# A state-space layer before a weight stream: where ScalarE's copies of C, its coefficient copy and two groups of TensorE products stand in the order of work

## The chip, the cores and the metric

The program runs on one core of a Trainium2 chip. Its time is the device time in microseconds (us) of that core, the median of three runs. TensorE is called PE here, VectorE DVE, ScalarE ACT, GpSimd POOL; SP is the engine that issues most DMA transfers. Each engine works through its own instructions strictly in the order in which the program wrote them, and waits at an instruction until what that instruction needs is there.

## What is computed

A decoder trunk of two layers on a sequence of 256 positions with 2048 channels. The first layer is a diagonal complex state-space model (128 groups of 16 channels, 64 states each) with a gated linear unit, then a feed-forward block; the second is dilated attention with a feed-forward block. The change touches the state-space part only:

```
u = rms_norm(x, a_norm_mix);  lb = exp(lam * dt);  f = (lb - 1) / lam
xs[s] = lb * xs[s-1] + (f * B) @ u[s]            # complex state, per group
y = Re(C @ xs) + d * u;  z = gelu(y)
x = x + (z @ w_glu)[:, :2048] * sigmoid((z @ w_glu)[:, 2048:])
x = x + swiglu(rms_norm(x), w_in, w_out)         # and then the second layer
```

## The kernel before, in words

The sequence is cut in 64 chunks of four positions. For the 64 pairs of groups (four *quarters* of 16 pairs, two *halves* of 32) the kernel builds small matrices: W, which takes four inputs into a chunk's end state; K, which takes inputs to outputs within a chunk; T, K laid out for a product with the inputs; and Q, which takes a chunk's start state to its outputs. C stands in the tile `ct` in three parts: minus imaginary, real, imaginary.

All orders are written out by hand. The body of `s5` (from L664) is the order of the state-space layer:

- **POOL**: `c_gain(k)` multiplies quarter k of C by the factor f (three operations of L236 to L238), `scale_u(k)` normalises a quarter of the inputs (L433), `q_build(k)` builds Q of quarter k (twelve operations of the same lines), and `l1([3], pool)` does one level of the scan for quarter 3 (L550 to L553).
- **ACT** copies: after each `c_gain` the negated part of C for that quarter (L465); after every group of transposes `v_trans(u)` the transposed W (L494); after every `v_build(u)` the chunk states `vs` (L509); after `k_build(h)` the matrix K of half h (L528); in `coefs(h, b)` the powers of the decay into a PSUM bank (L575); and the Gelu of the outputs (L634).
- **DVE**: eight times `w_build` (16 operations each, L139), then the scan over chunks: `l1([0, 1])`, `l2(0)`, `l3(0)`, `l3(1)`, `l1([2])`, `l2(1)`, `l3(2)`, `l3(3)` (L550 to L553, and L139 in `l2`). Every step of `l1` and `l3` on DVE reads the coefficients which `coefs` put into PSUM.
- **PE**: for each eighth u the transposes `v_trans(u)` (L151) and the products `v_build` (L505); `k_build(0)` in front of `v_trans(4)` and `k_build(1)` behind `v_build(7)` (L518, L523); `t_part(k)`, products of T with the inputs (L616); `s_part(k)`, products of Q with the scanned states (L628); `z_part(k)`, transposes of the Gelu's output (L151); and between these the first products of the weight stream (`plain`, L792), which `next(st)` advances.
- **SP**: two copies per `scale_u`, sixteen per `t_build(h)` (L536, K into T), and the loads of the weights (L858), 1 MB each, into three buffers that hold W until `k_build` and `v_trans` have read it.

After the state-space layer comes the weight stream: products at full size, with ACT and DVE splitting each weight tile into a high and a low part ahead of them.

Tiles with one tag take turns in a fixed number of buffers, and a new tile is written only after the last reader of the old one in its buffer. `hi` and `lo` have three each. The fourth `hi` tile, `wT[0]` (L472), follows the parameter tile `par`, whose last readers are L331 and L332 on POOL. The fifth `lo` tile, `wT[1]`, follows a tile of small values read last at L334. The fifth `hi` tile, `kt`, follows another tile of small values, read last by `scale_u(3)`.

Of the kernel before, what the change touches and what calls it, by code (L numbers as in the profile page):

```python
# [94 lines left out]
def bc(ap, shape, axes):  # L95
    for a in axes:
        ap = ap.unsqueeze(a)
    return ap.broadcast_to(list(shape))


class Trunk:
# [36 lines left out]
    def tt(self, out, in0, in1, op):  # L138
        self.nc.vector.tensor_tensor(out, in0, in1, op)  # L139
# [227 lines left out]
    def s5(self, st):  # L367
# [3 lines left out]
        upp, usw, bt, ct, vs, za, zb = self.upp, self.usw, self.bt, self.ct, self.vs, self.za, self.zb  # L371
# [33 lines left out]
        def wt(k, q0, n=1):  # L405

            w, q0 = (ws[3][q0 // 8], q0 % 8) if k == 3 else (ws[k], q0)
            return w[:, 128 * q0:128 * (q0 + n)].rearrange("p (q r j c) -> p q r j c", q=n, r=2, j=4)
# [13 lines left out]
        for m in range(2):  # L422
            h = rhs[:, 80 * m:80 * m + 80]
# [16 lines left out]
        fx = self.s5_gain(pool)  # L440
# [12 lines left out]
        def c_mul(o, x, k):  # L453

            qs = slice(16 * k, 16 * k + 16)
            sh = [128, 2, 16, 16]
            v4 = lambda v: v.rearrange("p (r q c) -> p r q c", r=2, q=16)
            self.cmul(pool, o, bc(x[:, 0, qs], sh, [1, 3]), bc(x[:, 1, qs], sh, [1, 3]), ct[:, 1:3, qs], ct[:, 0:2, qs],
                      v4(ptmp[0]), v4(ptmp[1]))

        def c_gain(k):

            qs = slice(16 * k, 16 * k + 16)
            c_mul(ct[:, 1:3, qs], fx, k)
            nc.scalar.activation(ct[:, 0, qs], ct[:, 2, qs], AF.Copy, scale=-1.0)  # L465

        def q_build(k):

            for t in range(4):
                c_mul(qv[k][:, :, :, 16 * t:16 * t + 16], self.lam[:, t, 1:3], k)  # L470
# [27 lines left out]
        def v_build(u):  # L498

            q0, e = 8 * u, u % 2  # L500
            pv = [self.bank(2 + ri) for ri in range(2)]
            for i in range(8):
                for ri in range(2):
                    for g2 in range(2):
                        nc.tensor.matmul(pv[ri][half(g2), 64 * i:64 * i + 64], wT[e][half(ri), i, half(g2)],  # L505
                                         (upp if ri == g2 else usw)[half(ri), q0 + i, 0:64], start=True, stop=True,
                                         tile_position=(64 * ri, 64 * g2))
            for ri in range(2):
                nc.scalar.copy(vs[:, ri, q0:q0 + 8], pv[ri].rearrange("p (q n) -> p q n", q=8))  # L509
# [3 lines left out]
        def k_build(h, bs):  # L513

            kk = [self.bank(b)[:, 0:256] for b in bs]
            c = lambda g2: slice(512 * h + 256 * g2, 512 * h + 256 * g2 + 256)
            for g2 in range(2):
                nc.tensor.matmul(kk[g2], self.ident, dm[:, c(g2)], start=True, stop=False)  # L518
            for i in range(16):
                for ri in range(2):  # L520
                    for i2 in range(2):
                        for g2 in range(2):
                            nc.tensor.matmul(kk[g2][half(i2), 16 * i:16 * i + 16],  # L523
                                             wt(2 * h + i2, i)[half(g2), 0, ri].rearrange("p j c -> p (j c)"),
                                             ct[half(g2), 1 + ri, 32 * h + 16 * i2 + i], start=False,
                                             stop=(i == 15 and ri == 1), tile_position=(64 * g2, 64 * i2))
            for g2 in range(2):
                nc.scalar.copy(kt[:, c(g2)], kk[g2])  # L528

        def t_build(h):  # L530

            for jp in range(4):
                s_ = 16 * (3 - jp)
                for g2 in range(2):
                    for i2 in range(2):
                        nc.sync.dma_start(th[h][64 * g2:64 * g2 + 64 - s_, jp, 256 * i2:256 * i2 + 256],  # L536
                                          kt[64 * i2 + s_:64 * i2 + 64, 512 * h + 256 * g2:512 * h + 256 * g2 + 256])
# [34 lines left out]
        def coefs(h, b):  # L572

            cps[h] = self.bank(b)[:, 0:384].rearrange("p (k r q) -> p k r q", k=4, r=3)
            nc.scalar.copy(cps[h], self.cpa[:, :, :, 32 * h:32 * h + 32])  # L575
# [15 lines left out]
        def l3(k):  # L591

            return pipe([level(k, slice(1, 16), slice(16 * i + 1, 16 * i + 16), i - 1, dve, i) for i in range(1, 4)], True)

        def go(ops, others=()):

            n = 0
            for i, f in enumerate(ops):
                while n < len(others) and n * len(ops) <= i * len(others):
                    others[n]()  # L600
                    n += 1
                f()
            for f in others[n:]:
                f()
# [4 lines left out]
        def t_part(k, bs):  # L609
            py = [self.bank(b) for b in bs]  # L610
            for e in range(2):
                for i in range(4):
                    for h in range(2):
                        q = 16 * k + 8 * e + 4 * h + i
                        for g2 in range(2):
                            nc.tensor.matmul(py[g2][half(h), 64 * (4 * e + i):64 * (4 * e + i) + 64], upp[half(g2), q, 16:80],  # L616
                                             th[k // 2][half(g2), :, 16 * (q % 32):16 * (q % 32) + 16],
                                             start=(e == 0 and i == 0), stop=False, tile_position=(64 * g2, 64 * h))
            return py

        def s_part(k, py):
            for e in range(2):
                for i in range(4):
                    for ri in range(2):
                        for h in range(2):
                            q = 8 * e + 4 * h + i
                            for g2 in range(2):
                                nc.tensor.matmul(py[g2][half(h), 64 * (4 * e + i):64 * (4 * e + i) + 64],  # L628
                                                 vs[half(g2), ri, 16 * k + q], qv[k][half(g2), ri, q], start=False,
                                                 stop=(e == 1 and i == 3 and ri == 1), tile_position=(64 * g2, 64 * h))  # L630
            z = upp[:, 16 * k:16 * k + 16, :].rearrange("p q n -> p (q n)")[:, 0:1024]
            z = z.rearrange("p (j i g c) -> p j i g c", j=4, i=8, g=2)
            for g in range(2):
                nc.scalar.activation(z[:, :, :, g].rearrange("p j i c -> p i j c"),  # L634
                                     py[g].rearrange("p (i j c) -> p i j c", i=8, j=4), AF.Gelu_apprx_tanh)
            zs[k] = z.rearrange("p j i g c -> p j (i g c)")
# [3 lines left out]
        def z_part(k, bs, plain):  # L640

            lo = []
            for e in range(2):
                pt = self.bank(bs[e])
                for j in range(4):
                    self.tr(pt[:, 128 * j:128 * j + 128], zs[k][:, j, 128 * e:128 * e + 128])
                v = lambda x, e=e: x.rearrange("p k (j n) -> p k j n", j=4)[:, 2 * e:2 * e + 2]
                src = pt.rearrange("p (j h n) -> p h j n", j=4, h=2)
                if plain:
                    nc.scalar.copy(v(full(k)), src)  # L650
                else:
                    hi, low = [v(self.zv(k, hl)) for hl in range(2)]
                    nc.scalar.copy(hi, src)
                    lo.append(lambda low=low, src=src, hi=hi: tt(low, src, hi.bitcast(F32), sub))
            return lo
# [11 lines left out]
            scale_u(k)  # L667
        for k in range(2, 4):
            c_gain(k)
        q_build(0)  # L670
        q_build(1)
        for u in range(8):
            go(w_build(u // 2, 8 * (u % 2), 8))
            if u == 4:
                v_build(3)
                k_build(0, (0, 1))
                t_build(0)
                coefs(0, 5)
            v_trans(u, (0, 1))
            if u not in (0, 4):  # L680
                v_build(u - 1)
        v_build(7)
        k_build(1, (2, 3))
        next(st)
        t_build(1)
        go(l1([0, 1], dve))
        py = [t_part(0, (0, 1))]
        py.append(t_part(1, (2, 3)))
        go(l1([3], pool))
        q_build(2)  # L690
        q_build(3)
# [3 lines left out]
        coefs(1, 4)  # L695
        go(l3(0))
        s_part(0, py[0])
        z_part(0, (0, 1), True)
        go(l3(1))
        next(st)  # L700
# [505 lines left out]
```

## Time and profile before

| | us |
|---|---|
| time, median of three runs (2216.51 to 2218.11) | 2217.62 |
| the profiled execution's own time | 2219.6 |
| its span, first to last instruction | 2217.8 |
| PE busy in the span | 2130.8 (96%) |
| DVE busy | 1523.4 (69%) |
| ACT busy | 1000.5 (45%) |
| POOL busy | 202.9 (9%) |

A busy share is a mean over the whole span, and most of the span is the weight stream. The state-space layer lies in about the first 157 us. The page cuts the span into 40 slices of 55.4 us; PE's busy tenths there are 0, 7, 9, 9 and so on, those of POOL 8, 8, 2, 1 and then 0. The mean granted TensorE clock of the execution is 0.990 of full speed.

### The profile page before, as it was taken

How to read it: one execution, taken by the hardware profiler on the slowest of the kernel's cores; microseconds unless marked ns; L12 is line 12 of the kernel's file. 1: busy time of each engine (PE TensorE's matmuls, PEld its weight loads, DVE VectorE, ACT ScalarE, POOL GpSimd, SP SyncE). 2: the span in 40 equal slices, each digit the busy share in tenths (PEclk: the TensorE clock that was granted, in tenths of full speed). 3: DMA queues.
4: the chain of work that ended last, by engine and by line, in shares of the span. 5: the costliest groups of instructions: out<-in, count | busy, mean ns of one | idle time of the engine just before them, and what ended most of it. 6: DMA issues, size and time to landing. Idle time of an engine off the chain costs nothing.

```text
span 2217.8 us, 28488 instructions
## 1 busy us (share of the span) xinstructions
PE 2130.8 (96%) x11132; PEld 1757.3 (79%) x11132; DVE 1523.4 (69%) x2621; ACT 1000.5 (45%) x1159; POOL 202.9 (9%) x180
## 2 busy tenths in 40 slices
PE   0799999999999999999999999999999999999998
PEld 0658888888888888878888888878888888888886
DVE  6686777677767764655776676687767776774544
ACT  2324444444444443434445555545444444444443
POOL 8821000000000000000000000000000000000000
PEclk9799999999999999999999999999999999999999
DMA  5235555555555555555554354445555555555553
GB/s 179 84 137 201 183 201 190 206 190 188 196 190 196 189 202 191 180 198 184 205 181 161 142 185 148 152 164 197 190 193 190 190 197 200 190 210 206 192 190 133
DMA packets 66839, 404.69 MB, mean 182 GB/s; under 512 B 15248, under 2 KB 16784, under 8 KB 19088
## 3 DMA queue, kind: packets, MB, share of 16 engines
q1 hardware_dynamic: 65696, 397.12, 50.9%
q10 hardware_dynamic: 720, 4.18, 0.5%
q8 instruction: 87, 1.43, 0.3%
q0 software_dynamic: 288, 1.57, 0.2%
q14 instruction: 48, 0.39, 0.1%
HBM read 397.34 MB, written 2.10 MB: 180 GB/s over the span
## 4 chain that ended last, share of the span: by engine, by line
PE 89%; DVE 6%; issue 2%; POOL 2%; ACT 1%; DMA 0%; ACTq 0%; POOLq 0%
PE b L778 28%; PE b L781 28%; PE b L777 28%; DVE scr L871 2%; DVE lo L139 1%; PE b L792 1%; PE b L151 1%; PE b L1094 1%; ACT hi L755 1%; PE b L1125 1%; POOL xw L433 1%; PE b L628 0%; PE b L1096 0%; PE b L1095 0%; DVE b L139 0%
## 5 line engine op out<-in xcount | busy, mean ns | idle before, releaser
L148 DVE SCALAR_TENSOR_TENSOR lo<-raw,gcol,hi 128x1024 fp32r<-128x1024 f32 x464 | 594.5, 1291 | 324.7 <-ACT hi L759 318.8
L777 PE MATMUL b<-hi,xt 128*128 128x512 f32 x1856 | 727.6, 392 | 1.3 <-ACT hi L759 1.3
L778 PE MATMUL b<-lo,xt 128*128 128x512 f32 x1856 | 724.2, 390 | 0.9 <-DVE lo L148 0.9
L759 ACT ACTIVATE hi<-raw,gcol 128x1024 fp32r<-128x1024 f32 x464 | 525.1, 1148 | 399.1 <-PE b L781 379.6
L781 PE MATMUL b<-hi,xt 128*128 128x512 f32 x1856 | 572.9, 390 | 0.0
L139 DVE TENSOR_TENSOR lo<-raw,hi 128x1024 fp32r<-128x1024 f32 x264 | 327.4, 1246 | 283.5 <-ACT hi L755 278.6
L755 ACT CAST hi<-raw 128x1024 fp32r<-128x1024 f32 x264 | 275.0, 1052 | 303.0 <-PE b L781 293.6
L781 PEld LDWEIGHTS b<-hi,xt 128*128 128x128 f32 x1856 | 349.1, 188 | 72.9
L777 PEld LDWEIGHTS b<-hi,xt 128*128 128x128 f32 x1856 | 348.8, 188 | 73.2 <-ACT hi L759 1.8
L778 PEld LDWEIGHTS b<-lo,xt 128*128 128x128 f32 x1856 | 349.3, 188 | 71.9 <-DVE lo L148 1.6
L778 PE MATMUL b<-lo,ht 128*128 128x512 f32 x704 | 274.7, 390 | 2.5 <-DVE lo L139 2.5
L777 PE MATMUL b<-hi,ht 128*128 128x512 f32 x704 | 274.4, 390 | 0.1
L871 DVE STREAM_TRANSPOSE scr<-scr 32x128 f32<-32x128 f32 x704 | 212.9, 302 | 11.4
L781 PE MATMUL b<-hi,ht 128*128 128x512 f32 x704 | 217.4, 390 | 0.0
L778 PEld LDWEIGHTS b<-lo,ht 128*128 128x128 f32 x704 | 132.3, 188 | 31.3 <-DVE lo L139 4.1
L777 PEld LDWEIGHTS b<-hi,ht 128*128 128x128 f32 x704 | 132.2, 188 | 27.8 <-ACT hi L755 0.5
L781 PEld LDWEIGHTS b<-hi,ht 128*128 128x128 f32 x704 | 132.2, 188 | 27.3
L875 POOL TENSOR_TENSOR ht<-scr,ht 128x512 fp32r<-128x512 f32 x44 | 57.0, 1295 | 880.9 <-ACT ht L874 880.9
L874 ACT CAST ht<-scr 128x512 fp32r<-128x512 f32 x44 | 27.3, 621 | 178.6 <-DVE scr L871 178.6
L871 DVE STREAM_TRANSPOSE scr<-x 32x128 f32<-32x128 f32 x320 | 96.8, 302 | 4.9
L875 POOL TENSOR_TENSOR xt<-scr,xt 128x512 fp32r<-128x512 f32 x20 | 25.9, 1294 | 769.9 <-ACT xt L874 642.0
L778 PE MATMUL b<-lo,z 128*128 128x512 f32 x224 | 87.7, 392 | 0.6 <-DVE lo L139 0.6
(207 smaller groups left out, 1463.1 us busy)
## 6 DMA issues: line engine op xcount, KB each, us to landing
raw<-in_fi SPq DMA_DIRECT2D x176, 1024.0 KB, 4.7
raw<-in_fo SPq DMA_DIRECT2D x88, 1024.0 KB, 4.7
raw<-in_wq SPq DMA_DIRECT2D x48, 1024.0 KB, 4.7
raw<-in_glu SPq DMA_DIRECT2D x32, 1024.0 KB, 4.8
raw<-in_wo SPq DMA_DIRECT2D x16, 1024.0 KB, 4.8
raw<-in_kv SPq DMA_DIRECT2D x8, 1024.0 KB, 4.7
xw<-in_xu SPq DMA_DIRECT2D x4, 640.0 KB, 11.1
qp<-in_xr SPq DMA_DIRECT2D x4, 512.0 KB, 9.7
```

The source lines that it names most:

```text
L139: self.nc.vector.tensor_tensor(out, in0, in1, op)
L148: self.nc.vector.scalar_tensor_tensor(out, in0, s, in1, op0, op1)
L151: self.nc.tensor.transpose(out, in_, self.ident[:n, :n])
L433: pool.tensor_tensor(upp[:, qs, :], upp[:, qs, :], bc(rt, [128, 16, 80], [1]), mul)
L755: nc.scalar.copy(hi, raw)
L759: nc.scalar.activation(hi, raw, AF.Copy, scale=gk)
L777: nc.tensor.matmul(ps[b], xh, hi[:, c], start=first, stop=False)
L778: nc.tensor.matmul(ps[b], xh, lo[:, c], start=False, stop=False)
L781: nc.tensor.matmul(ps[b], xl, hi[:, c], start=False, stop=last)
L871: nc.vector.transpose(out[32 * q:32 * q + 32, :, 32 * a:32 * a + 32], src[32 * a:32 * a + 32, :, q, :])
L874: nc.scalar.copy(dst(0), out)
L875: nc.gpsimd.tensor_tensor(dst(1), out, dst(0).bitcast(F32), ALU.subtract)
```

## The change

`c_gain` no longer has its ACT copy. A new function `c_turn(h)` makes the copies of two quarters in one instruction; its two calls stand behind `t_build(0)` and behind `v_build(7)`. `q_build(0)` and `q_build(1)` are written behind `c_turn(1)`. `coefs(0, 5)` moves from u = 4 to u = 2. On PE `t_part(0)` stands ahead of `k_build(1)`, and `t_part(1)` behind `s_part(0)`.

```diff
         def c_gain(k):
 
-            qs = slice(16 * k, 16 * k + 16)
-            c_mul(ct[:, 1:3, qs], fx, k)
+            c_mul(ct[:, 1:3, 16 * k:16 * k + 16], fx, k)
+
+        def c_turn(h):
+
+            qs = slice(32 * h, 32 * h + 32)
             nc.scalar.activation(ct[:, 0, qs], ct[:, 2, qs], AF.Copy, scale=-1.0)
...
         for k in range(2, 4):
             c_gain(k)
-        q_build(0)
-        q_build(1)
         for u in range(8):
             go(w_build(u // 2, 8 * (u % 2), 8))
             if u == 4:
                 v_build(3)
                 k_build(0, (0, 1))
                 t_build(0)
-                coefs(0, 5)
+                c_turn(0)
             v_trans(u, (0, 1))
             if u not in (0, 4):
                 v_build(u - 1)
+            if u == 2:
+                coefs(0, 5)
         v_build(7)
+        c_turn(1)
+        q_build(0)
+        q_build(1)
+        py = [t_part(0, (0, 1))]
         k_build(1, (2, 3))
         next(st)
         t_build(1)
         go(l1([0, 1], dve))
-        py = [t_part(0, (0, 1))]
-        py.append(t_part(1, (2, 3)))
         go(l1([3], pool))
...
         s_part(0, py[0])
+        py.append(t_part(1, (2, 3)))
         z_part(0, (0, 1), True)
```

## Rows read from the trace of the kernel before

**Rows 1.** Waits, 15 to 160 us: who waited for whom, total, times, longest (us).

```profile
DVE b L550 <- ACT b L575: 28.8, 1, 28.8
ACT z L465 <- POOL z L238: 26.7, 4, 12.0
```

**Rows 2.** Timeline of ACT: start, us, engine, line, operation, [idle before <- releaser].

```profile
52.37 0.42 ACT L465 ACTIVATE z<-z 128x256 f32<-128x256 f32 x1 [3.07 <-POOL z L238]
52.69 1.05 ACT L494 COPY hi<-b 128x512 f32<-128x512 f32 x2
...
64.81 1.07 ACT L509 COPY vs<-b 128x512 f32<-128x512 f32 x2 [1.17 <-PE b L505]
72.03 0.65 ACT L528 COPY hi<-b 128x256 f32<-128x256 f32 x2 [6.15 <-PE b L523]
72.56 0.50 ACT L575 COPY b<-scr 128x384 f32<-128x384 f32 x1
```

**Rows 3.** Timeline of DVE.

```profile
43.60 0.75 DVE L139 TENSOR_TENSOR z<-b,hi 128x256 f32<-128x256 f32 x2
73.10 0.70 DVE L550 TENSOR_TENSOR b<-b,vs 128x512 f32<-128x512 f32 x1 [28.76 <-ACT b L575]
...
108.18 0.67 DVE L550 TENSOR_TENSOR b<-b,vs 128x480 f32<-128x480 f32 x1
...
123.71 0.27 DVE L139 TENSOR_TENSOR b<-b,vs 128x64 f32<-128x64 f32 x1
...
143.82 0.66 DVE L553 TENSOR_TENSOR vs<-b,hi 128x480 f32<-128x480 f32 x1
```

**Rows 4.** Timeline of PE.

```profile
85.02 1.19 PE L518 MATMUL b<-lo,cst 128*128 128x256 f32 x4 [0.60 <-ACT vs L509]
...
95.47 3.84 PE L616 MATMUL b<-tz,xw 64*64 64x64 f32 x126
108.29 3.71 PE L628 MATMUL b<-qp,vs 64*64 64x64 f32 x128 [8.99 <-DVE vs L553]
113.17 1.97 PE L151 MATMUL b<-cst,xw 128*128 128x128 f32 x8 [1.18 <-ACT xw L634]
...
119.75 2.10 PE L628 MATMUL b<-qp,vs 64*64 64x64 f32 x128
...
144.74 2.09 PE L628 MATMUL b<-qp,vs 64*64 64x64 f32 x127
148.49 0.27 PE L628 MATMUL b<-qp,vs 64*64 64x64 f32 x1 [1.66 <-issue]
...
154.88 2.05 PE L628 MATMUL b<-qp,vs 64*64 64x64 f32 x128
```

**Rows 5.** Timeline of POOL.

```profile
31.30 0.45 POOL L332 TENSOR_TENSOR lo<-hi,lo 128x128 f32<-128x128 f32 x1
...
39.76 5.72 POOL L433 TENSOR_TENSOR xw<-xw,hi 128x1280 f32<-128x1280 f32 x2
...
53.43 1.06 POOL L237 TENSOR_TENSOR lo<-scr,z 128x512 f32<-128x512 f32 x1
...
79.08 1.29 POOL L238 TENSOR_TENSOR qp<-lo 128x512 f32<-128x512 f32 x1
85.60 1.05 POOL L550 TENSOR_TENSOR lo<-scr,vs 128x512 f32<-128x512 f32 x1 [5.23 <-ACT vs L509]
...
98.16 1.20 POOL L553 TENSOR_TENSOR vs<-lo 128x480 f32<-128x480 f32 x1
...
126.14 1.27 POOL L238 TENSOR_TENSOR qp<-lo 128x512 f32<-128x512 f32 x1
```

**Rows 6.** Timeline of SP: issues of the first sixteen copies of K.

```profile
72.43 12.03 SPq L536 DMA_DIRECT2D tz<-hi  x16
```

**Rows 7.** DMA issues by line: count, KB each, median us from issue to landing.

```profile
tz<-hi SPq DMA_DIRECT2D x8, 64.0 KB, 2.0
```

**Rows 8.** By stretch: us, busy time of each engine, granted clock, DMA share, GB/s.

```profile
108.30:113.00 4.70, 3.70 (x128) 3.51 (x128) 4.63 (x9) 0.96 (x2) 4.46 (x5) 0.50 0.08 17
```

## The prediction

> **What bounds the kernel now.** I read the 40 slices first: PE is busy nine tenths and more from the third slice on, so the weight stream is bound by PE, and nothing in the change touches an instruction of it. What the change can move is the moment at which the stream takes over, some 157 us after the start. So I took the waits of 15 to 160 us next. Two of them are long [rows 1]: DVE waits 28.8 us, once, for the coefficients that ACT copies, and ACT waits 26.7 us, in four pieces, for POOL's products of C. The timelines show that they are one chain. ACT's copy for quarter 3 of C (52.37 us) waits for POOL, and the copies of W stand behind it and begin at 52.69; from there PE, ACT and PE again go through transposes, states and K, until ACT, behind the copies of K (72.03 + 0.65), copies the coefficients at 72.56 [rows 2]. DVE has built the last W at 43.60 + 0.75 = 44.35 and stands until 73.10 [rows 3]. From 73.10 it runs without a gap through l1, l2(0) and l3(0), and s_part(0) on PE starts at 108.29, released by DVE after 8.99 us of idle time [rows 4]. So POOL's products of C hold ACT, ACT holds DVE, DVE holds PE, and PE starts the rest late.
>
> **The change part by part.**
>
> *The copies of C leave ACT's queue ahead of W.* The first copy of W no longer waits for 52.37 + 0.42. The next thing that it waits for is its buffer: `wT[0]` takes the one of `par`, read last on POOL by L332, which ends at 31.30 + 0.45 = 31.75 [rows 5]. So the copies of W begin at about 31.8, which is 52.69 - 31.75 = 20.9 earlier. PE's and ACT's work from there is the same, and I shift it as it stands: the states of v_build(3), copied by 64.81 + 1.07 = 65.88 [rows 2], are there at 45.0. Their operands don't hold them: DVE finishes all eight parts of W at 44.35, when only the fourth is used here, and quarters 0 and 1 of the inputs stand ahead of L332 in POOL's order. k_build(0) then needs quarter 1 of C, finished when POOL goes on to the next row at 39.76 [rows 5]; PE gets there at 64.81 - 20.9 = 43.9.
>
> *The coefficients at u = 2.* They add their 0.50 [rows 2] to ACT between two copies that PE waits for; I add all of it: states of v_build(3) at 45.4, copies of K at 72.68 - 20.9 + 0.5 = 52.2. DVE finds the coefficients ready when it has built W at 44.35. It needs the states of quarter 0 first and those of quarter 1 only with its fourth operation, some 1.8 us later (46.2, operations of about 0.6), after 45.4. So its scan starts at 44.35 in place of 73.10, **28.75 us earlier**, and this is the main term [rows 3]. Nothing on DVE can give more, since the 44.35 stays.
>
> *c_turn.* Half of C in one copy lies between the 0.42 of a quarter and the 1.05 of two tiles of 512 columns; I take 0.6, nearest to half of the latter [rows 2]. c_turn(0) ends at 52.2 + 0.6 = 52.8. It adds a wait to POOL: q_build(0) is behind it, and with q_build(0) all that POOL does later. The first operation of q_build(0) that reads the negated part started at 53.43 [rows 5], so it loses nothing, with 0.6 us to spare. c_turn(1), behind v_build(7), is needed by q_build(2) alone, far later.
>
> *POOL after that.* q_build(1) ends where it did, 79.08 + 1.29 = 80.37. Then l1 of quarter 3 waited 5.23 us, until 85.60, for the states of v_build(7); these come 20.4 earlier (20.9 less the coefficients' 0.5), at 65.2, and the wait goes. l1 takes 98.16 + 1.20 - 85.60 = 13.76 and ends at 94.1. DVE's l2(1) needs it; its start moves from 123.71 to 94.96 [rows 3, 5]. The cover is thin, 0.8 us, but it holds. q_build(3) ends at 126.14 + 1.27 - 5.23 = 122.2; s_part(3), moved by some 28 from 154.88 [rows 4, 5], needs it at about 127.
>
> *t_part(0) ahead of k_build(1).* On PE this adds a wait for SP's sixteen copies of K. They took 12.03 us to issue and the large ones land after 2.0 [rows 6, 7]: from 52.2 to 64.3, landed at 66.3. The states of v_build(7), which PE waited for until 85.02, come 20.4 earlier, at 64.6, so PE stands some 2 us. Behind it are k_build(1), then the third weight load and the second sixteen copies on SP. t_part(0) takes half of the pair's 3.84, 1.9; k_build(1) with its start took 95.47 - 85.02 = 10.45, a pause of PE's own in it. It ends at 66.3 + 1.9 + 10.45 = 78.7, and s_part(0) can start at 108.29 - 28.75 = 79.5 [rows 4]. So this costs nothing, by 0.8 us; without that cover each us later costs one.
>
> *t_part(1) behind s_part(0).* It lay in PE's idle time; now 1.9 us stand on PE's path, beside a wait of 1.18 for the Gelu [rows 4]. So 0.74 is added, between 0 (quick products, which the Gelu covers whole) and 1.9 (if the Gelu is late by as much). z_part(0) is behind it, and behind that the first weight products.
>
> *From s_part(0) to the stream* PE hardly stands, and its instructions are the same. l3(2) ends at 143.82 + 0.66 = 144.48 - 28.75 = 115.7; PE, which reached s_part(2) at 144.74, gets there at 144.74 - 28.75 + 0.74 = 116.7 [rows 3, 4]. So PE sets this, by 1.0, and the sum is -28.75 + 0.74 = **-28.0 us**.
>
> This sum takes s_part(0) at its slow length: 3.71, where s_part(1) takes 2.10, with a granted clock of 0.50 from 108.30 to 113.00, the lower level of 1.2 GHz, after 9 us in which PE stood [rows 4, 8]. In the changed kernel PE stands less before it. The Trainium skill, page "TensorE: Matmul & The Clock Gate", Part 1, says that "the default state is throttled, and activity releases the throttle". By that rule s_part(0) may run at 2.4 GHz; by the row it ran at 1.2 after an idle stretch longer than the one that I expect, so the row leaves it open, and I make it a rival.
>
> The profiled execution took 2219.6, the span of 2217.8 and 1.8 around it; that is 2.0 above the median of 2217.62. 2219.6 - 28.0 = 2191.6, and by the median **2189.6**.
>
> **The rivals.**
>
> *A quicker clock at s_part(0).* If s_part(0) takes 2.10 and t_part(1) hides behind the Gelu, PE comes to s_part(2) at least 1.61 + 0.74 sooner. But then l3(2) is late: s_part(2) starts at 115.7 and not before, 144.74 - 115.7 = 29.0 saved, 2188.6. For it: less idle time before. Against: 0.8 us of pause and whatever slow stretch k_build(1) itself has. If the pause of 1.66 that PE makes at the end of s_part(2) [rows 4] went too, it would be 30.7, 2186.9, the bottom of what I can construct.
>
> *POOL becomes the bound.* If PE pauses in k_build(0), or waits there for more of C than it reads, c_turn(0) comes late. From 55.2 on (53.43, the cover of 0.8 and the 1.0 by which DVE is ahead of PE) each us costs one. If k_build(0) had to wait for quarter 3 of C, 52.4 in place of 43.9 [rows 2], c_turn(0) would end at 52.8 + 8.5 = 61.3: 6.1 lost, -21.9, 2195.7. For it: the covers are thin. Against: DVE's l1 of quarters 0 and 1 ran from 73.10 [rows 3] while states of later quarters in the same tile were being written, so waits follow the part that is read.
>
> *The copies of W don't start at 31.8.* If their buffers were held until scale_u(3) has read its factors, at 39.76 + 5.72 = 45.48 [rows 5], 13.7 later, the states of quarter 1 would come at 45.4 + 13.7 = 59.1, where DVE wants them at 46.2: 12.9 lost, -15.1, 2202.5. By the count of three buffers it is `kt` that waits for that reader, and not `wT`.
>
> *The wait on DVE stays*, if something else of that chain holds the states until 73: then no more than t_part(1)'s 0.74 is changed, 2218.4.
>
> *Slower: q_build behind c_turn(0).* POOL's whole rest, 28 us of q_build, 13.8 of l1 and 28 of q_build, now hangs on one ACT copy that is queued behind the copies of K. From 55.2 on it eats the gain, and from 55.2 + 28.0, about 83, the kernel is slower. If it were done only after k_build(1)'s end of before, 95.5 + 0.6 = 96.1 [rows 4], the kernel would be 12.9 slower, 2230.5. Against: even at the times of before the copies of K ended at 72.68 [rows 2], ten us short of that point.
>
> **How the numbers follow.** My forecast 0.66, quicker clock 0.14, POOL as the bound 0.10, late copies of W 0.05, the wait stays 0.03, slower 0.02. The range is 2186.5 to 2196.0: it holds the first three, 0.90 together, less what the sizes in them leave uncertain, about 0.8. Below it is only the bottom of the second; 2196.0 takes in thin covers that fail by up to 6 us. A measurement of this kernel tells 0.2%, 4.4 us, from no change: faster 0.95, same 0.03, slower 0.02.
>
> **What would show it.** DVE's first L550 near 44.4 in place of 73.1, with no wait for L575; the first W copy of ACT near 31.8; POOL's first L237 of q_build still near 53.4; no 5.23 before POOL's L550, and l2(1) near 95; PE with a wait before t_part(0) at about 64 to 66, k_build(1) done before 79.5, s_part(0) released by DVE at 79.5 and then t_part(1). From s_part(2) on all should lie some 28 us earlier. I am wrong if DVE still waits before l1, if PE comes late to s_part(0) because of k_build(1), or if l2(1) waits for POOL.

## The result, and the profile after

The changed kernel takes 2192.55 us (median of four runs, 2190.69 to 2192.97) against 2217.79 for the kernel before (four runs, 2216.51 to 2218.11): a ratio of 0.9886, 95% interval 0.9869 to 0.9903, 25.2 us faster. The forecast was 28.0 faster, at 2189.6, with a range from 2186.5 to 2196.0. The profiled execution took 2192.67, with a span of 2190.9; the one of the kernel before took 2219.6, with a span of 2217.8. By either number these two executions differ by 26.9.

The chain that was to break is broken at its first link. This is ACT's timeline, which answers to [rows 2] (line numbers have moved, by 3 up to the Gelu and by 6 in the weight stream: L497 was L494, L512 was L509, L531 was L528, L553 to L556 were L550 to L553, L578 was L575, L619 was L616, L631 was L628, L798 was L792; L468 is `c_turn`).

```profile
31.81 1.07 ACT L497 COPY hi<-b 128x512 f32<-128x512 f32 x2 [7.36 <-POOL lo L332]
...
39.57 0.50 ACT L578 COPY b<-scr 128x384 f32<-128x384 f32 x1
...
43.21 1.07 ACT L512 COPY vs<-b 128x512 f32<-128x512 f32 x2 [1.17 <-PE b L508]
50.53 0.65 ACT L531 COPY hi<-b 128x256 f32<-128x256 f32 x2 [6.25 <-PE b L526]
51.06 0.65 ACT L468 ACTIVATE z<-z 128x512 f32<-128x512 f32 x1
```

The copies of W start at 31.81 in place of 52.69, and what they now wait for is L332 on POOL, the last reader of the buffer. The coefficients are there at 40.1, the states of v_build(3) at 44.3. DVE's timeline answers to [rows 3]:

```profile
43.63 0.74 DVE L139 TENSOR_TENSOR z<-b,hi 128x256 f32<-128x256 f32 x2
44.48 0.70 DVE L553 TENSOR_TENSOR b<-b,vs 128x512 f32<-128x512 f32 x1
...
95.22 0.27 DVE L139 TENSOR_TENSOR b<-b,vs 128x64 f32<-128x64 f32 x1
...
115.39 0.66 DVE L556 TENSOR_TENSOR vs<-b,hi 128x480 f32<-128x480 f32 x1
```

The wait of 28.76 us is gone: no bracket stands behind the first L553. POOL, to be held against [rows 5], has lost its wait of 5.23 in front of l1 (L553, L550 before). Up to there its work lies within 0.3 us of where it was, and behind it everything is some 5 us earlier:

```profile
53.59 1.06 POOL L237 TENSOR_TENSOR lo<-scr,z 128x512 f32<-128x512 f32 x1
...
80.63 1.06 POOL L553 TENSOR_TENSOR lo<-scr,vs 128x512 f32<-128x512 f32 x1
...
93.22 1.21 POOL L556 TENSOR_TENSOR vs<-lo 128x480 f32<-128x480 f32 x1
```

PE's timeline, beside [rows 4]:

```profile
63.84 1.28 PE L619 MATMUL b<-tz,xw 64*64 64x64 f32 x62 [0.36 <-DMA tz<-hi]
...
79.80 3.69 PE L631 MATMUL b<-qp,vs 64*64 64x64 f32 x128 [3.48 <-DVE vs L556]
83.24 1.46 PE L619 MATMUL b<-tz,xw 64*64 64x64 f32 x64
84.67 1.09 PE L151 MATMUL b<-cst,xw 128*128 128x128 f32 x8
86.00 3.70 PE L798 MATMUL b<-raw,xw 128*128 128x512 f32 x8 [0.24 <-ACT xw L653]
...
116.19 2.09 PE L631 MATMUL b<-qp,vs 64*64 64x64 f32 x127 [1.50 <-DVE vs L556]
119.47 0.27 PE L631 MATMUL b<-qp,vs 64*64 64x64 f32 x1 [1.20 <-issue]
120.43 1.09 PE L151 MATMUL b<-cst,xw 128*128 128x128 f32 x8 [0.69 <-ACT xw L637]
121.36 5.29 PE L798 MATMUL b<-raw,xw 128*128 128x512 f32 x8
126.58 1.16 PE L619 MATMUL b<-tz,xw 64*64 64x64 f32 x64
127.56 2.05 PE L631 MATMUL b<-qp,vs 64*64 64x64 f32 x128
129.54 0.50 PE L783 MATMUL b<-hi,z 128*128 128x512 f32 x1
```

Three more rows of the kernel before belong beside these: the weight products behind s_part(0) and behind s_part(2), and the first product of the weight stream.

```profile
114.97 4.86 PE L792 MATMUL b<-raw,xw 128*128 128x512 f32 x8
...
150.37 3.60 PE L792 MATMUL b<-raw,xw 128*128 128x512 f32 x8
...
156.86 0.50 PE L777 MATMUL b<-hi,z 128*128 128x512 f32 x1
```

s_part(0) starts 28.49 us earlier than before, s_part(2) 28.55, the transposes behind it 29.01, but s_part(3) only 27.32 (154.88 less 127.56). What differs between the last two is one row: eight weight products that take 5.29 us, where the same eight took 3.60 before. The views by stretch show why; the columns are those of [rows 8], the granted clock the number in front of the DMA share. First the kernel before, then the changed one:

```profile
149.40:150.30 0.90, 0.86 (x8) 0.86 (x9) 0.87 (x2) 0.11 (x1) 0.00 (x0) 1.00 0.09 18
150.30:153.90 3.60, 3.60 (x11) 1.41 (x8) 3.33 (x5) 2.85 (x4) 0.00 (x0) 1.00 0.00 0
```

```profile
79.80:83.50 3.70, 3.70 (x140) 3.70 (x143) 3.63 (x7) 0.00 (x0) 3.62 (x4) 0.50 0.40 117
83.50:86.00 2.50, 2.26 (x72) 1.92 (x66) 2.43 (x5) 1.72 (x4) 2.34 (x3) 0.90 0.23 59
...
119.40:121.30 1.90, 1.14 (x9) 1.01 (x10) 1.87 (x4) 0.70 (x2) 1.82 (x3) 1.00 0.03 9
121.30:126.60 5.30, 5.30 (x14) 2.00 (x11) 5.20 (x8) 2.86 (x4) 1.18 (x1) 0.68 0.00 0
```

The clock comes up sooner behind s_part(0), in 83.5 to 86.0, and falls for a part of 121.3 to 126.6 (0.50 in 122.5 to 124.0), after PE stood three times in a row: 1.50 for DVE, 1.20 of its own, 0.69 for the Gelu. From s_part(3) on the two executions run side by side again: the stream starts 27.32 earlier (129.54 for 156.86) and takes 0.4 longer, which leaves 26.9 at the end of the span.

### The profile page after: what moved, and what is told of

It is laid out like the page before. It is cut to its first block, busy times and chain, and to the rows that moved or that the text cites. A ratio compares the mean times of both kernels' runs of the same rounds, so it can differ in the third digit from the quotient of the medians.

```text
span 2190.9 us, 28487 instructions
## 1 busy us (share of the span) xinstructions
PE 2129.8 (97%) x11132; PEld 1754.8 (80%) x11132; DVE 1523.6 (70%) x2621; ACT 999.6 (46%) x1157; POOL 203.6 (9%) x180
## 4 chain that ended last, share of the span: by engine, by line
PE 88%; DVE 9%; issue 2%; ACT 1%; DMA 0%; ACTq 0%; DVEq 0%
PE b L784 28%; PE b L783 28%; PE b L787 28%; DVE scr L877 2%; DVE lo L139 1%; DVE b L139 1%; PE b L151 1%; PE b L1100 1%; ACT hi L761 1%; DVE b L553 1%; PE b L1131 1%; DVE b L555 1%; DVE vs L556 1%; DVE hi L554 0%; DVE hi L139 0%
## 5 line engine op out<-in xcount | busy, mean ns | idle before, releaser
L880 ACT CAST ht<-scr 128x512 fp32r<-128x512 f32 x44 | 27.3, 621 | 178.6 <-DVE scr L877 178.6
```

Source lines behind the costliest of these rows:

```text
L880: nc.scalar.copy(dst(0), out)
```

## The experiments

All are edits of the changed kernel, timed against the kernel before on the same chip. That kernel's median was 2218.60 beside the runs whose labels begin with `a_` to `d_`, 2218.12 beside `e_turn_late`, `g_w_sixteen` and `dg_both`, and 2219.02 beside `h_half_first` and `gh_both`. The ratios' intervals are about 0.0015 to either side, some 3 us: runs that lie within 3 us of each other are told apart by the rows of their traces, not by their times. Each trace is one execution.

**The coefficients late again** (`a_coefs_late`)

```diff
                 t_build(0)
+                coefs(0, 5)
                 c_turn(0)
...
-            if u == 2:
-                coefs(0, 5)
```

> The changed kernel with one part undone: coefs(0, 5) stands behind the copies of K again, ahead of c_turn(0). My theory (DVE's first scan step waits for the later of W, states and coefficients, and the whole rest follows DVE): the copies of K end at 50.7, the coefficients at 51.2, the scan starts there and not at 44.5, so 6.7 us are lost, 2199.3. Rival, the copies of C alone bring the gain: the time of the changed kernel, 2192.6.

Measured: 2200.78, ratio 0.9919 (0.9906 to 0.9933). DVE's timeline:

```profile
51.58 0.70 DVE L553 TENSOR_TENSOR b<-b,vs 128x512 f32<-128x512 f32 x1 [7.19 <-ACT b L578]
```

The scan starts 7.1 later than in the changed kernel (6.7 expected), and s_part(0) (86.82) and s_part(2) (123.22) are 7.0 later. The profiled execution, 2199.98, is 7.3 above that of the changed kernel. The rival, that the copies of C alone bring the gain, would have left 2192.6: it falls.

**The copies of C back in ACT's queue** (`b_copies_back`)

```diff
             c_mul(ct[:, 1:3, 16 * k:16 * k + 16], fx, k)
+            qs = slice(16 * k, 16 * k + 16)
+            nc.scalar.activation(ct[:, 0, qs], ct[:, 2, qs], AF.Copy, scale=-1.0)
...
-                c_turn(0)
...
-        c_turn(1)
```

> The changed kernel with the negated copies of C back in c_gain, a quarter at a time, and without c_turn; the coefficients stay early. My theory: ACT's copies of W wait for POOL until 52.7 again, the states of quarter 1 come at 65.2, and the fourth scan operation runs there in place of 46.3: 18.9 us are lost, 2211.5. Rival, the early coefficients alone bring the gain: 2192.6.

Measured: 2212.28, ratio 0.9968 (0.9955 to 0.9980).

```profile
61.82 0.70 DVE L555 TENSOR_TENSOR b<-b,vs 128x512 f32<-128x512 f32 x1 [17.49 <-ACT b L580]
...
66.03 0.70 DVE L555 TENSOR_TENSOR b<-b,vs 128x512 f32<-128x512 f32 x1 [2.32 <-ACT vs L514]
```

The first operation waits for the coefficients, which ACT now delivers at 61.8, and the fourth for the states, which come at 66.0: 19.7 later than the fourth operation at 46.28 in the changed kernel. s_part(0) starts at 99.52, 19.7 later too. So neither edit does it alone: coefficients early without the copies moved give about 6 of the 25 us, copies moved without early coefficients about 18.

**The T products where they were** (`c_t_order_back`)

```diff
-        py = [t_part(0, (0, 1))]
         k_build(1, (2, 3))
...
         go(l1([0, 1], dve))
+        py = [t_part(0, (0, 1))]
+        py.append(t_part(1, (2, 3)))
...
         s_part(0, py[0])
-        py.append(t_part(1, (2, 3)))
```

> The changed kernel with both t_part behind k_build(1) and ahead of s_part(0) again. My theory: no difference beyond 1 us, 2191.6 to 2193.6, since k_build(1) with its pauses still ends ahead of the scan's 79.8 and s_part(2) waits for DVE anyway. Rival, the order of the T products is part of the gain: k_build(1) and both t_part end behind 79.8 and s_part(0) is late by 1 to 3 us, 2194 to 2196.

Measured: 2191.83, ratio 0.9877 (0.9864 to 0.9891): the same, as far as this can tell. The rows show that two things cancel.

```profile
76.09 3.94 PE L619 MATMUL b<-tz,xw 64*64 64x64 f32 x126
79.81 0.35 PE L631 MATMUL b<-qp,vs 64*64 64x64 f32 x9
83.06 3.48 PE L631 MATMUL b<-qp,vs 64*64 64x64 f32 x119 [2.89 <-issue]
...
117.66 2.09 PE L631 MATMUL b<-qp,vs 64*64 64x64 f32 x127
...
122.93 3.60 PE L798 MATMUL b<-raw,xw 128*128 128x512 f32 x8
```

Both t_part end at 80.0, just in time. But a pause of PE's own, 2.89, now falls into s_part(0), which ends at 86.54, 3.05 later than in the changed kernel. So far the rival is right. The changed kernel has no such pause there; why it comes here is not shown. s_part(2) comes at 117.66, 1.5 later, without a wait for DVE; behind it the clock stays at 1.00 (122.9 to 126.5), the weight products take 3.60, and s_part(3) starts at 127.44, within 0.12 of the changed kernel. So in these two executions the order of the T products is worth nothing at the end of the stage, though my reason (s_part(2) waits for DVE anyway) was not what happened.

**c_turn(0) late** (`e_turn_late`)

```diff
-                c_turn(0)
...
+        c_turn(0)
         v_build(7)
         c_turn(1)
```

> The changed kernel with c_turn(0) put in front of v_build(7), so that it ends at 62.2 and not at 51.7. This tests the cover on POOL. My theory: the first read of the negated part in q_build(0) moves from 53.6 to 62.2, POOL's l1 of quarter 3 ends 8.6 later, at 103.0, and DVE's l2(1), with 0.8 us of cover, starts at 103.1 in place of 95.2; nothing behind it takes that up, so 7.8 us are lost, 2200.4. Rival, POOL is hidden (it is 9% busy): 2192.6.

Measured: 2200.15, ratio 0.9918 (0.9905 to 0.9932). POOL's timeline, then DVE's:

```profile
63.52 1.06 POOL L237 TENSOR_TENSOR lo<-scr,z 128x512 f32<-128x512 f32 x1 [9.90 <-ACT z L468]
...
103.10 1.20 POOL L556 TENSOR_TENSOR vs<-lo 128x480 f32<-128x480 f32 x1
```

```profile
104.33 0.28 DVE L139 TENSOR_TENSOR b<-b,vs 128x64 f32<-128x64 f32 x1 [9.27 <-POOL vs L556]
```

POOL, busy in 9% of the span, stops the kernel: the copy came 1.3 later than I had reckoned, l2(1) is 9.1 late and s_part(2) (125.25) as well. 1.1 of it comes back: the weight products behind s_part(2) take 3.60 in place of 5.29 (1.69), 0.97 less lies between s_part(2) and the transposes, where PE's own pause of 1.20 is not there, and s_part(2) itself, at a granted clock of 0.54, takes 3.61 in place of 2.09 (1.52 lost); s_part(3) at 135.48 is 7.9 late. That the time comes so near to the 2200.4 expected is in part luck: the 1.3 too much and the 1.1 that came back nearly cancel.

**The last weight step ahead of s_part(2)** (`d_weights_first`)

```diff
+        next(st)
         s_part(2, py[2])
...
         lo = z_part(2, (2, 3), False)
-        next(st)
```

> The changed kernel with the last step of unsplit weight products (n = 7) put ahead of s_part(2), where PE stood 1.5 us for DVE. My theory (the wait for l3(2) and the pauses behind it are PE time lost, and the granted clock fell behind them): s_part(2) starts at 118.2 without a wait, the stream at 127.1 in place of 129.5, so 2190.2, with the clock at its upper level all through. Rival: the pause between s_part(2) and z_part(2) is longer without these products, the clock falls all the same: 2192 to 2193.

Measured: 2189.12, ratio 0.9865 (0.9850 to 0.9881).

```profile
117.75 2.10 PE L631 MATMUL b<-qp,vs 64*64 64x64 f32 x128
121.03 1.09 PE L151 MATMUL b<-cst,xw 128*128 128x128 f32 x8 [1.19 <-ACT xw L637]
...
123.52 1.70 PE L619 MATMUL b<-tz,xw 64*64 64x64 f32 x59 [1.07 <-DVE vs L556]
```

```profile
123.50:125.00 1.50, 1.48 (x61) 1.48 (x65) 1.15 (x2) 1.26 (x2) 0.00 (x0) 0.59 0.00 0
125.00:128.10 3.10, 3.10 (x141) 3.03 (x135) 2.41 (x4) 0.00 (x0) 0.00 (x0) 0.65 0.24 53
```

The wait in front is gone and the stream starts at 128.02 in place of 129.54, but not at the 127.1 that I expected: without weight products behind s_part(2) PE stands 1.19 there and again until DVE's scan ends, and the clock falls all the same. On this the rival was right; the time is below both, 1.1 under my 2190.2 and 2.9 under the rival's 2192.

**W in wider operations** (`g_w_sixteen`), and both edits together (`dg_both`)

```diff
-            go(w_build(u // 2, 8 * (u % 2), 8))
+            if u >= 6:
+                go(w_build(3, 8 * (u % 2), 8))
+            elif u % 2 == 0:
+                go(w_build(u // 2, 0, 16))
```

> The changed kernel with W of quarters 0 to 2 built by operations of 512 columns in place of two of 256 each (same numbers of W). By 0.60 for 512 columns and 0.335 for 256, DVE is done 1.9 us sooner, at 42.5, and the scan starts there. My theory: s_part(0) moves by 1.9, but l2(1) then waits for POOL's l1 of quarter 3, which stays at 94.4, so only 0.8 us reach s_part(2): 2191.7. Rival, DVE alone sets the rest: 1.9 us, 2190.6.

> The weight products ahead of s_part(2) and W in operations of 512 columns, both. My theory: behind s_part(2) the T products of quarter 3 wait for the end of DVE's scan, which POOL lets come 0.8 us sooner: 0.8 below the run with the weight products moved alone (2189.1), so 2188.3. Rival, DVE alone: 1.9 below it, 2187.2.

Measured: 2188.93 (2188.20 to 2191.13), ratio 0.9870 (0.9856 to 0.9883), and 2190.12, ratio 0.9873 (0.9859 to 0.9886). DVE's timeline in the first:

```profile
40.81 0.74 DVE L139 TENSOR_TENSOR z<-b,hi 128x256 f32<-128x256 f32 x2
...
44.54 0.70 DVE L553 TENSOR_TENSOR b<-b,vs 128x512 f32<-128x512 f32 x1 [0.98 <-ACT vs L512]
...
94.18 0.27 DVE L139 TENSOR_TENSOR b<-b,vs 128x64 f32<-128x64 f32 x1 [0.73 <-POOL vs L556]
```

DVE is done with W 2.8 us sooner (41.55; 1.9 expected), then waits 0.98 for the states of quarter 1 and 0.73 for POOL. s_part(0) starts at 78.13, 1.7 earlier, and s_part(2) at 115.11, 1.1 earlier. So POOL passes on 1.1, nearer to my 0.8 than to the rival's 1.9. In the profiled execution the clock fell here as well, already in s_part(2) (0.62 in 115.1 to 118.3, 0.50 behind it), and the stream starts at 128.40, the same 1.1 earlier; its time is the 2191.13, and the others lie 2 to 3 us below. Their median is 2.8 under the 2191.7 expected and 1.7 under the rival's, and no row shows why. With both edits the stream starts at 127.01 (0.2 before what I expected), yet the time is 1.8 above the 2188.3 expected; from its start to the end of the span the stream took 2061.1 there and 2060.3 with the weight step moved alone, and what that 0.8 is stays open. The same stretch took 2061.4 in the changed kernel and 2060.9 in the kernel before, so differences of this size come with any two executions compared here.

**The last weight step cut in two** (`h_half_first`), and with W in wider operations (`gh_both`)

```diff
+        next(st)
         s_part(2, py[2])
...
-        for n in range(2, self.PLAIN):
+        for n in range(2, self.PLAIN - 1):
             plain(n, (0, 1))
             yield
+        for m in range(2):
+            plain(self.PLAIN - 1, (m,))
+            yield
```

> The changed kernel with the last unsplit step of weight products (n = 7) cut in two: the products for the first 128 positions ahead of s_part(2), those for the second behind z_part(2). My theory (the clock fell because PE stood before s_part(2) and again behind it, and an idle stretch of PE filled on both sides keeps it up): 1.8 us of products fill the 1.5 in front of s_part(2) and 1.8 the time until DVE's scan ends at 123.5; s_part(2) at 116.5, s_part(3) at 124.7, the stream from 126.8, against 129.5 in the changed kernel and 128.0 with the whole step in front: 2188.9 for an execution with the clock at 1.00 from 113 to 129. Rival, the clock falls by chance of the moment and not for the idle time: 2190 to 2192 with a stretch at 0.50.

> The same with W in operations of 512 columns. My theory: POOL lets 0.8 us of DVE's gain through, so the stream starts at 126.0, 2188.1. Rival, PE sets the end of this stretch by then: as the run with the step cut in two alone.

Measured: 2189.47 (2188.66 to 2189.60), ratio 0.9867 (0.9850 to 0.9883), and 2188.05 (2187.85 to 2188.88), ratio 0.9861 (0.9846 to 0.9876). The first by stretch and on PE:

```profile
112.00:129.00 17.00, 15.14 (x353) 10.24 (x352) 14.96 (x23) 6.07 (x9) 10.36 (x10) 1.00 0.47 156
```

```profile
116.87 2.10 PE L631 MATMUL b<-qp,vs 64*64 64x64 f32 x128
120.16 1.09 PE L151 MATMUL b<-cst,xw 128*128 128x128 f32 x8 [1.19 <-ACT xw L637]
121.08 1.88 PE L799 MATMUL b<-raw,xw 128*128 128x512 f32 x4
```

With work on both sides of s_part(2) the clock stays at its upper level, 2.4 GHz, all through, and the stream starts at 126.84, which is the 126.8 expected. Its profiled execution took 2188.66, 0.2 below what I had written; the other three took 2189.43 to 2189.60, and were not traced, so whether the clock held in them is not known. The median does not tell this run from the one with the whole step in front (2189.12); the 1.2 between them is read from two traces.

In the second the stream starts at 125.96 (126.0 expected), and PE still stands three times:

```profile
115.54 2.09 PE L631 MATMUL b<-qp,vs 64*64 64x64 f32 x128 [1.19 <-DVE vs L556]
118.81 1.09 PE L151 MATMUL b<-cst,xw 128*128 128x128 f32 x8 [1.18 <-ACT xw L637]
...
123.01 1.10 PE L619 MATMUL b<-tz,xw 64*64 64x64 f32 x59 [1.07 <-DVE vs L556]
```

```profile
112.00:128.00 16.00, 12.56 (x347) 9.02 (x346) 14.21 (x22) 5.99 (x9) 10.11 (x10) 1.00 0.35 122
```

These stops add up to 3.4 us, as do the three of the changed kernel (1.50, 1.20, 0.69), and the clock stays at 1.00: here half a weight step, 1.88, lies between the second and the third. Its median is 31.0 us below the kernel before, the lowest of all that ran; its interval overlaps those of its neighbours and that of the changed kernel.

## Why the prediction was right

*The copies of C.* Right. 31.8 was forecast for the first copy of W, 31.81 measured, released by L332 as the count of buffers said; so "the copies of W don't start at 31.8" falls, and "the wait on DVE stays" with it.

*The main term.* Right: 44.35 forecast, 44.48 measured. The runs with either edit undone show that the scan goes on only when both the coefficients and the states are there, and that the rest follows it.

*c_turn and POOL.* Right: 0.65 for 0.6, done at 51.7 for 52.8; q_build reads at 53.59, l1 of quarter 3 ends at 94.43 for 94.1, l2(1) starts at 95.22 for 94.96. The cover of 0.8 is what the trace has, and the run with c_turn(0) late shows the price behind it. The rival "POOL becomes the bound" and the one that ends slower rest on this mechanism, and it exists; only the point from which it decides was not reached. That point lies sooner than the 55.2 of the prediction: of its terms the 1.0 by which DVE was to be ahead of PE is not there (see below), which leaves 53.59 + 0.79 = 54.4. With c_turn(0) late the first read came at 63.52, 9.1 behind that, and l2(1) was 9.1 late.

*t_part(0).* Its wait was mis-sized: 0.36 us in place of 2. SP was through with its issues 1.5 sooner (50.92 + 11.91 = 62.83, from SP's timeline), and PE went on at 63.84, where I had the copies landed at 66.3. k_build(1)'s copies start at 76.35, where I had 78.7; the cover was larger than I said.

*t_part(1).* 0.74 forecast, nothing measured: the transposes behind it start 1.18 after s_part(0) ends, as before. It took 1.46 and not 1.9; the granted clock rose in it (0.78 in 83.5 to 84.6, 1.00 behind that).

*From s_part(0) to the stream.* Here the forecast has its error, in the path as well as in size. "PE sets this, by 1.0" failed. The rival of a quicker clock came half true: s_part(0) itself took 3.69, at 0.50, but what follows took 1.09 and 3.70 where the kernel before had 1.97 [rows 4] and 4.86, at a clock that stayed at 0.50 until 117.0. By the Trainium skill, page "TensorE: Matmul & The Clock Gate", Part 1, activity releases the throttle; the trace agrees, 0.50 until 83.5 and 0.90 behind it, with less idle time ahead. So s_part(1) starts 9.83 behind s_part(0) in place of 11.46, and PE, 1.6 quicker here, was through with the work ahead of s_part(2) at 114.69, where the forecast had 116.7, and DVE set the start. s_part(2) came 28.55 earlier, where the rival had 29.0. That the transposes behind it are 29.01 earlier is no hit of the rival's: 0.46 of it is PE's own pause, 1.20 in place of 1.66. What no case of mine had is the other half: behind PE's three stops there the clock fell again, and the products took 5.29 in place of 3.60, 1.7 us. So it is in part luck that the 28.0 of the sum and the 27.3 at the stream's start lie so near: s_part(2) gained 0.5 more than the sum, and 1.2 was lost behind it. The same page, section "HAM oscillation — how this bites in real kernels", describes a kernel whose waits between groups of products throw it back to the lower clock. The rows here agree that the clock falls behind such waits, but not on their length: each wait there, by the page some 3 to 5 us, is longer than any of the three here (1.50, 1.20, 0.69). The run with the step cut in two, with the wait in front filled and the others at 1.19 and 0.67, has 1.00 throughout. That the stops are the cause is thus likely, not shown: it rests on one execution of each kernel, and the last section has a case of three stops without a fall.

*From the span to the median.* 27.3 at the stream's start and 26.9 at its end are 0.7 and 1.1 less than the 28.0. The rest of the way to 25.2 is not in the trace: the execution that was profiled before lay 1.8 above its kernel's median, the one after 0.1. I had applied the difference of the first to the second unchanged. That the runs of one kernel spread by 2 us is the limit of any sum made from one of them. Where the spread comes from is not shown: each kernel has one trace, and the mean granted clock does not go with the time (with the T products moved back, the fastest execution, 2190.13, has the lowest clock, 0.992).

## What to carry to other kernels

A short copy that waits for a slow engine costs little itself (0.42 us here); what it costs stands behind it in its queue, so look at what the next engine down the chain is waiting for, and follow it until the waiting stops: here POOL, ACT, DVE, PE. When such a chain is cut, ask at once which engine has the least cover next (POOL had 0.8 us; at s_part(2) PE was 1.5 early and DVE had none), since the gain ends there, and one more copy in the wrong place gives a third of it back. Where PE waits for another engine between short groups of products, spread what independent products there are over both sides of the wait rather than all on one: in the traces that brought the stream's start forward by 1.2 us against all in front, too little to show in the times.

## What the runs showed of the hardware

- In the changed kernel the granted clock fell from 1.00 to 0.50 after PE stood 1.50, 1.20 and 0.69 us within 6 us, which cost 1.7 us; in the kernel before it did not after 1.66 and 0.69 [rows 4]. In two more traces with a wait for DVE in front it fell too (1.39, 1.46 and 0.69 with the coefficients late; 1.28, 1.61 and 0.69 with the copies of C back), and in one without it, with 1.30 and 0.69 (T products moved back), it stayed at 1.00. But the count of stops does not decide: the clock fell after two, 1.19 and 1.07, with the weight step in front, and stayed at 1.00 through three, 1.19, 1.18 and 1.07, with the step cut in two and W wider. What decides stays open.
- PE pauses of its own inside long runs of very short products: 1.80 and 3.18 us in the two k_build of the changed kernel, and 2.89 in s_part(0) when both t_part stood ahead of it. The 3.18 begins while 1 MB weight loads are under way (269 GB/s in 63.0 to 67.3). But such loads are not needed for a pause: the 0.99 in the first k_build of the kernel before (68.69 to 69.68) and the 1.20 in s_part(2) of the changed kernel (118.28 to 119.47) both came with the DMA engines at 0.00. What causes the pauses stays open.
